# The mixer's output projection as seven products of block sums instead of eight block products

## The chip, the cores and the metric

One core of a Trainium2 chip runs the whole program. The metric is device time in microseconds (us) of that core. The kernel before was run three times: 1793.5, 1794.19 and 1794.78 us, median 1794.19 us. Each number of the trace comes from one profiled execution of its own.

## The reference, cut to what matters

Two layers of an encoder over 512 tokens with 1024 features, in f32. The change touches the one line marked in this cut; the lines around it say what is made before it and used after it.

```python
def reference(x, p, w_in, ...):
    h = x
    for i in range(DEPTH):
        u = rms_norm(h, norm_mix_pre[i])
        ...
        merged = (jax.nn.sigmoid(gate_a) * (att @ w_att_out[i])
                  + jax.nn.sigmoid(gate_b) * (ret @ w_ret_out[i]))
        h = h + rms_norm(merged @ w_out[i], norm_mix_post[i])      # the projection of the change
        u = rms_norm(h, norm_mlp_pre[i])
        ff = jnp.square(jax.nn.relu(u @ w_mlp_up[i])) @ w_mlp_down[i]
        h = h + rms_norm(ff, norm_mlp_post[i])
        gate = jax.nn.sigmoid(rms_norm(h) @ w_ple_gate[i])
        h = h + gate * rms_norm(p[i] @ w_ple_proj[i], norm_ple[i])
    return h
```

`merged` is 512 tokens x 1024 features, `w_out[i]` is 1024 x 1024.

## The kernel before, in words

**Precision.** Every f32 operand of a matmul is kept as two parts, a high part (rounded to the type that TensorE multiplies, made by a copy on ScalarE) and a low part (the rest, made by a subtraction on VectorE or GpSimd). A product takes three matmuls (high by high, high by low, low by high: `HL`, line 295).

**Weights.** All weights lie in HBM as chunks of 128 x 1024 numbers (512 KB). `PLAN_LAYER` (line 69) writes out the order of the chunks of a layer; `_items` (line 93) turns it into the items that TensorE uses. `prefetch` (line 271) prepares up to three items ahead of the one in use: SyncE's queue loads the chunk (`raw`, line 254), ScalarE makes the high part (line 278), VectorE or, for some kinds, GpSimd in two halves, the low part (line 301). Five tiles `wt` hold prepared items, so a new one can be begun when the item five before it has been used. Where an item is a sum of two blocks (so far only in the MLP's down projection, which already is done as seven products), `total` (line 260) loads one block with SyncE's queue into a tile and adds the other with an accumulating DMA that GpSimd issues (line 268). Raw chunks sit in four tiles of the tag "R", sums in two tiles of the tag "X".

**Order.** TensorE's instructions run in the order in which the program gives them. Those of the other engines are put in order by the scheduler, by priority, which is the place in the program; what is wrapped in `soon` (line 375) gets a higher one. Each engine then works its list in that order. `step` (line 325) counts pieces of work of TensorE, six matmuls each in the stages of interest, and after a fixed count (`AGE` 7, `AGE_PP` 8) puts waiting transposes into TensorE's order.

**The stage of the change (lines 753 to 777).** The eight feature tiles of `merged`, transposed, lie in `fb`; each gets its last addend from GpSimd (line 752). They are split into `uT` (lines 753 to 755). Then `row_job` (line 332) makes the left 512 columns of the product for all four token tiles (`ALL`), and then the right 512 columns one token tile after another (`ONES`): 192 matmuls of 512 columns. `evac_wo` (line 761) takes each result out of PSUM: sum of squares on ScalarE, product with the gain on VectorE. When a token tile t is complete, `pre_norm` (line 393) makes the norm's factor (two small GpSimd operations, lines 359 and 361), the residual (two VectorE operations, line 773), two sums of squares on ScalarE, another factor on GpSimd and the normalized rows `un` (two VectorE operations, line 406). Its `rest` (line 408) transposes `un` on TensorE in two PSUM banks of the tag "tp", of which there are two in all, and splits them into `uT` again (ScalarE line 416, VectorE line 417).

**After it.** `pp` (lines 786 to 797): 48 matmuls of 512 columns in eight pieces that don't need the norm, evacuated in turn by VectorE and ScalarE (`pn`). Then the first three chunks of the MLP's up projection, first for tokens 0 to 255 and then for 256 to 511 (`early`, lines 862 to 875), which do need `uT` of those tokens.

```python
    def row_mm(ps, ch, j, lhs, k, t, first, last):
        for n, (a, b) in enumerate(HL):
            nc.tensor.matmul(ps, lhsT=lhs(a, k, t), rhs=ch[:, b, j * S:(j + 1) * S],
                             start=first and n == 0, stop=last and n == 2)

    def step(age=None):
        clock[0] += 1
        age = AGE if age is None else age
        if pending and clock[0] - pending[0][0] >= age:
            soon(pending.pop(0)[1])()
        tick()
```

## Time and profile before

| what | value |
|---|---|
| three runs, median | 1794.19 us |
| profiled execution: its time | 1794.64 us |
| profiled execution: span of the trace | 1792.9 us |
| TensorE (PE) busy, matmuls | 1772.4 us (99% of the span), 8209 |
| VectorE (DVE) busy | 1145.4 us (64%) |
| ScalarE (ACT) busy | 807.5 us (45%) |
| GpSimd (POOL) busy | 382.6 us (21%) |
| DMA | 274.58 MB, mean 153 GB/s |

The time of the execution is 1.7 us above the span, which runs from the first to the last instruction. PE's granted clock is at its full level in all slices of the span. The rows name tiles by the program's names: `wt` prepared weights, `raw` and `wsum` weights on their way, `acc`, `s` and `tp` PSUM banks (and `acc` also the stage's result in SBUF), `un` normalized rows, `uT` transposed operands, `fT` the tiles of `merged`. A row of the timeline gives the start, the duration, engine, line, operation, tiles, count, and in brackets how long the engine was idle before and what released it.

### The profile page before, as it was taken

How to read it: one execution, taken by the hardware profiler on the slowest of the kernel's cores; microseconds unless marked ns; L12 is line 12 of the kernel's file. 1: busy time of each engine (PE TensorE's matmuls, PEld its weight loads, DVE VectorE, ACT ScalarE, POOL GpSimd, SP SyncE). 2: the span in 40 equal slices, each digit the busy share in tenths (PEclk: the TensorE clock that was granted, in tenths of full speed). 3: DMA queues.
4: the chain of work that ended last, by engine and by line, in shares of the span. 5: the costliest groups of instructions: out<-in, count | busy, mean ns of one | idle time of the engine just before them, and what ended most of it. 6: DMA issues, size and time to landing. Idle time of an engine off the chain costs nothing.

```text
span 1792.9 us, 22127 instructions
## 1 busy us (share of the span) xinstructions
PE 1772.4 (99%) x8209; PEld 1466.2 (82%) x8209; DVE 1145.4 (64%) x1803; ACT 807.5 (45%) x1271; POOL 382.6 (21%) x354
## 2 busy tenths in 40 slices
PE   8999999999999999999999999999999999999998
PEld 6888788888898888888788887888888888888887
DVE  6676777743465677674656767677444657667754
ACT  4255444332466454433443555444333664444342
POOL 2312244311142001002123222442012410000030
PEclk9999999999999999999999999999999999999999
DMA  5555464552347655552346545555422566664421
GB/s 213 194 193 159 149 212 137 166 175 95 117 142 188 165 158 161 156 184 70 129 141 214 165 145 172 184 159 187 136 101 99 165 170 156 169 175 130 165 71 60
DMA packets 87807, 274.58 MB, mean 153 GB/s; under 512 B 11921, under 2 KB 20497, under 8 KB 87698
## 3 DMA queue, kind: packets, MB, share of 16 engines
q1 hardware_dynamic: 80786, 247.99, 40.7%
q0 software_dynamic: 6912, 25.17, 8.3%
q8 instruction: 65, 1.06, 0.2%
q14 instruction: 44, 0.36, 0.1%
HBM read 239.55 MB, written 33.55 MB: 152 GB/s over the span
## 4 chain that ended last, share of the span: by engine, by line
PE 89%; DVE 4%; POOL 2%; ACT 2%; issue 1%; DMA 1%; SPq 0%; POOLq 0%; ACTq 0%
PE acc L312 28%; PE acc L322 19%; PE s L312 18%; PE acc L849 8%; PE tp L849 4%; PE tp L612 2%; PE tp L544 2%; PE tp L507 2%; PE acc L871 1%; PE tp L413 1%; POOL wt L301 1%; PE s L525 1%; PE s L526 1%; PE s L590 1%; PE s L871 1%
## 5 line engine op out<-in xcount | busy, mean ns | idle before, releaser
L312 PE MATMUL acc<-uT,wt 128*128 128x512 f32 x1920 | 472.8, 392 | 0.0
L312 PEld LDWEIGHTS acc<-uT,wt 128*128 128x128 f32 x1920 | 356.2, 188 | 71.8
L301 DVE TENSOR_TENSOR wt<-raw,wt 128x1024 fp32r<-128x1024 f32 x217 | 279.4, 1292 | 187.6 <-ACT wt L278 187.1
L278 ACT ACTIVATE wt<-raw 128x1024 fp32r<-128x1024 f32 x280 | 293.9, 1055 | 223.0 <-PE acc L312 114.0
L322 PE MATMUL acc<-wt,uT 128*128 128x512 f32 x1320 | 320.8, 396 | 4.4 <-ACT uT L416 1.8
L312 PE MATMUL s<-uT,wt 128*128 128x512 f32 x1392 | 323.7, 389 | 0.0
L312 PEld LDWEIGHTS s<-uT,wt 128*128 128x128 f32 x1392 | 261.1, 188 | 54.1
L322 PEld LDWEIGHTS acc<-wt,uT 128*128 128x128 f32 x1320 | 245.6, 189 | 55.6 <-DVE uT L417 2.6
L301 POOL TENSOR_TENSOR wt<-raw,wt 128x512 fp32r<-128x512 f32 x126 | 173.2, 1395 | 408.1 <-ACT wt L278 339.1
L849 PE MATMUL acc<-wt,op 128*128 128x512 f32 x672 | 159.5, 389 | 0.0
L849 PEld LDWEIGHTS acc<-wt,op 128*128 128x128 f32 x672 | 126.1, 188 | 26.2
L268 POOL DMA_DIRECT2D wsum<-in_w_dram x48 | 42.8, 900 | 420.1 <-DVE wt L301 141.0
L892 ACT ACTIVATE relu<-s 128x512 f32<-128x512 f32 x60 | 35.7, 595 | 180.7 <-PE s L312 172.0
L860 DVE TENSOR_TENSOR sumP<-acc,sumP 128x512 f32<-128x512 f32 x92 | 61.8, 686 | 56.4 <-PE acc L849 56.1
L312 PE MATMUL acc<-retT,wt 128*128 128x512 f32 x384 | 89.3, 389 | 0.0
L322 PE MATMUL acc<-wt,ff 128*128 128x512 f32 x384 | 88.5, 390 | 0.0
L301 DVE TENSOR_TENSOR wt<-wsum,wt 128x1024 fp32r<-128x1024 f32 x48 | 60.6, 1263 | 41.7 <-ACT wt L278 41.7
L312 PEld LDWEIGHTS acc<-retT,wt 128*128 128x128 f32 x384 | 72.1, 188 | 15.0
L322 PEld LDWEIGHTS acc<-wt,ff 128*128 128x128 f32 x384 | 71.8, 188 | 14.8
L304 ACT ACTIVATE rt<-rz 128x512 fp32r<-128x512 f32 x64 | 40.3, 631 | 91.5 <-DVE rz L594 91.0
L849 PE MATMUL tp<-wt,op 128*128 128x512 f32 x336 | 80.7, 389 | 0.0
L849 PEld LDWEIGHTS tp<-wt,op 128*128 128x128 f32 x336 | 63.1, 188 | 13.1
(165 smaller groups left out, 2153.5 us busy)
## 6 DMA issues: line engine op xcount, KB each, us to landing
raw<-in_w_dram SPq DMA_DIRECT2D x280, 512.0 KB, 3.7
wsum<-in_w_dram POOLq DMA_DIRECT2D x48, 512.0 KB, 5.5
kk<-stk SPq DMA_DIRECT2D x128, 128.0 KB, 3.8
wsum<-in_w_dram SPq DMA_DIRECT2D x24, 512.0 KB, 3.3
stq<-rr SPq DMA_DIRECT2D x16, 512.0 KB, 3.4
qs<-stq SPq DMA_DIRECT2D x128, 64.0 KB, 2.9
stk<-rr SPq DMA_DIRECT2D x16, 512.0 KB, 3.0
stv<-vr SPq DMA_DIRECT2D x16, 512.0 KB, 4.4
```

The source lines that it names most:

```text
L268: nc.gpsimd.dma_start(r, rows(src[1]), accum_op=ALU.add)
L278: nc.scalar.activation(t[:, 0, :], r, AF.Copy)
L301: eng.tensor_tensor(dst, src, hi.bitcast(F32), op=ALU.subtract)
L304: nc.scalar.activation(dst[:, 0], src, AF.Copy, scale=scale)
L312: nc.tensor.matmul(ps, lhsT=t[:, a, (off + k) * P:(off + k + 1) * P], rhs=r, start=k == 0 and n == 0, stop=k == kts - 1 and n == 2)
L322: nc.tensor.matmul(ps, lhsT=lhs(a, k, t), rhs=ch[:, b, j * S:(j + 1) * S], start=first and n == 0, stop=last and n == 2)
L507: nc.tensor.matmul(o, lhsT=v, rhs=pt[k][:, hl, :], start=k == 0 and hl == 0, stop=k == 3 and hl == 1)
L544: nc.tensor.transpose(ps[:, t * P:(t + 1) * P], zs[t][:, k * P:(k + 1) * P], ident)
L612: nc.tensor.matmul(o, lhsT=v[:, k, a * P:(a + 1) * P], rhs=rt[k][:, b, :], start=n == 0, stop=n == 11)
L849: nc.tensor.matmul(ps, lhsT=op[:, a, k, j * P:(j + 1) * P], rhs=t[:, b, k * S:(k + 1) * S], start=k == 0 and n == 0, stop=k == 1 and n == 2)
L860: nc.vector.tensor_tensor(a, ps, a, op=ALU.add)
L871: nc.tensor.matmul(early[c][:, 256 * j:256 * j + 256], lhsT=t[:, a, k * P:(k + 1) * P], rhs=uT[:, b, k, 256 * j:256 * j + 256], start=k == ...
```

## The change

The 512 x 1024 operand and the 1024 x 1024 weight are cut into two by two blocks, and the product is made as seven products of sums of blocks where eight block products were summed. Per layer and product: two items of weights (q), each used by twelve matmuls of 512 columns for two token tiles (j): 168 matmuls. The sums of weight blocks are made by accumulating DMAs as in the down projection; the first sum (P5) is kept in "R" tiles and grows into P6 and P4. The sums of the operand's blocks are made by VectorE (x, y, z, v), each operand is split (`wo_operand`), four of them into `uT`. The results are combined by VectorE in `evac_wo`. Tokens 256 to 511 (t = 2, 3) are complete after the sixth product (P4), tokens 0 to 255 after the seventh (P2). The early part of the up projection takes the second token half first.

```diff
-    + [("wo", c) for c in range(8)]
+    + [("wo", c) for c in (0, 1, 4, 5, 6, 7, 2, 3)]
...
+            if kind == "wo":
+                if c == 0:
+                    b11, b21, b12, b22 = ([CHUNK[i, "wo", 2 * b + q] for q in range(2)] for b in range(4))
+                    out += [((i, "wo" + p, q), tuple(b if b == "chain" else b[q] for b in src)) for p, src in (
+                        ("P1", (b11,)), ("P5", (b11, b12)), ("P6", ("chain", b22)), ("P7", (b12, b22)),
+                        ("P3", (b22,)), ("P4", ("chain", b21)), ("P2", (b21,))) for q in range(2)]
+                continue
...
     def total(key, src):
+        at = key[2] if key[1][:2] == "wo" else "sum"
         if src[0] == "chain":
-            r = chain["sum"]
+            r = chain[at]
         else:
-            r = blk("X", [P, D], name="wsum")
+            held = key[1][-2:] == "P5"
+            r = blk("R" if held and at != "sum" else "X", [P, D], name="wsum")
             nc.sync.dma_start(r, rows(src[0]))
-            if key[1] == "P5":
-                chain["sum"] = r
+            if held:
+                chain[at] = r
         nc.gpsimd.dma_start(r, rows(src[1]), accum_op=ALU.add)
...
-        for c in range(8):
-            src = fb[c // 2][:, c % 2, :]
-            split(uT[:, :, c, :], src)
...
+        def wo_operand(x, q, src, at=None):
+            if at is None:
+                at = blk("P", [P, 2, 2, 256], F32R, name="wop")
+            nc.scalar.activation(at[:, 0], src, AF.Copy)
+            nc.vector.tensor_tensor(at[:, 1], src, at[:, 0].bitcast(F32), op=ALU.subtract)
+            wop[x, q] = at
+
+        f1, f2 = fb[:2], fb[2:]
+        lo_k, hi_k = ([uT[:, :, 4 * kh + 2 * q:4 * kh + 2 * q + 2, :] for q in range(2)] for kh in range(2))
...
+        def sum_x(q, o):
+            nc.vector.tensor_tensor(o, f2[q][:, :, 256:], f1[q][:, :, 256:], op=ALU.subtract)
...
+        def sum_z(q, o):
+            nc.vector.tensor_tensor(o, f1[q][:, :, :256], f1[q][:, :, 256:], op=ALU.subtract)
...
+        def sum_y(q, o):
+            nc.vector.scalar_tensor_tensor(o, wx[q], -1.0, f1[q][:, :, :256], op0=ALU.mult, op1=ALU.subtract)
...
+        def sum_v(q, o):
+            nc.vector.scalar_tensor_tensor(o, wy[q], -1.0, f2[q][:, :, :256], op0=ALU.mult, op1=ALU.subtract)
...
+        for q in range(2):
+            wo_operand("P1", q, f1[q][:, :, :256], lo_k[q][:, :, :, :256])
+        wx = sums(sum_x)
+        wy = sums(sum_y)
+        for q in range(2):
+            wo_operand("P5", q, wx[q], lo_k[q][:, :, :, 256:])
+            wo_operand("P6", q, wy[q])
+        wz = sums(sum_z)
+        for q in range(2):
+            wo_operand("P7", q, wz[q])
+        wv = sums(sum_v)
+        for q in range(2):
+            wo_operand("P3", q, wv[q])
+        for q in range(2):
+            wo_operand("P4", q, f2[q][:, :, 256:], hi_k[q][:, :, :, 256:])
+        for q in range(2):
+            wo_operand("P2", q, f2[q][:, :, :256], hi_k[q][:, :, :, :256])
...
-        row_job([(i, "wo", c) for c in range(4)], u_lhs, evac_wo(0))
-        row_job([(i, "wo", 4 + c) for c in range(4)], u_lhs, evac_wo(1), ONES)
+        def done_wo(t, hf, src, eng):
+            hs_ = HALVES[hf]
+            ssq[t][hf] = sumsq(src, t2("junk"), None if hf else 1e-6)
+            eng.tensor_tensor(acc[t][:, hs_], src, g_post[:, hs_], op=ALU.mult)
+            if not hf:
+                pre_norm(h[t], t, g_pre, residual(t, acc, rstd_of(*ssq[t])))
...
+        @soon
+        def evac_wo(x, j, ps):
+            (l1, r1), (l2, r2) = ([a[:, sl] for sl in HALVES] for a in (acc[j], acc[2 + j]))
+            if x == "P1":
+                nc.scalar.activation(l1, ps, AF.Copy)
+            elif x == "P5":
+                w5.append(ps)
+            elif x == "P6":
+                nc.vector.tensor_tensor(l2, ps, l1, op=add)
+                nc.vector.tensor_tensor(r1, w5[j], l2, op=add)
+            elif x == "P7":
+                nc.vector.scalar_tensor_tensor(r2, ps, -1.0, r1, op0=ALU.mult, op1=ALU.subtract)
+                nc.vector.tensor_tensor(l2, ps, l2, op=add)
+                done_wo(2 + j, 1, r2, nc.gpsimd)
+            elif x == "P3":
+                nc.vector.scalar_tensor_tensor(r1, ps, -1.0, r1, op0=ALU.mult, op1=ALU.subtract)
+                done_wo(j, 1, r1, nc.gpsimd)
+            elif x == "P4":
+                nc.vector.tensor_tensor(l2, ps, l2, op=add)
+                done_wo(2 + j, 0, l2, nc.vector)
+            else:
+                nc.vector.tensor_tensor(l1, ps, l1, op=add)
+                done_wo(j, 0, l1, nc.vector)
+
+        w5 = []
+        wo_banks = [bank(tag) for tag in ("acc", "acc", "s", "s", "acc", "acc")]
+        for m, pr in enumerate(("P1", "P5", "P6", "P7", "P3", "P4", "P2")):
+            pss = [wo_banks[(2 * m + j) % 6] for j in range(2)]
+            for q in range(2):
+                t = chunk(i, "wo" + pr, q)
+                for j in range(2):
+                    for k in range(2):
+                        for n, (a, b) in enumerate(HL):
+                            nc.tensor.matmul(pss[j], lhsT=wop[pr, q][:, a, k, j * P:(j + 1) * P], rhs=t[:, b, k * S:(k + 1) * S],
+                                             start=q == 0 and k == 0 and n == 0, stop=q == 1 and k == 1 and n == 2)
+                    if q:
+                        evac_wo(pr, j, pss[j])
+                    step()
...
-        for j in range(2):
+        for j in (1, 0):
             settle(PAIRS[j])
             for c in range(EARLY):
-                if not j:
+                if j:
                     early.append(bank(EARLY_BANKS[c]))
```

## Rows read from the trace of the kernel before

**Rows 1.** Page part 1: engine, busy us, share of the span, instructions.

```profile
PE 1772.4 (99%) x8209; PEld 1466.2 (82%) x8209; DVE 1145.4 (64%) x1803; ACT 807.5 (45%) x1271; POOL 382.6 (21%) x354
```

**Rows 2.** Chain that ended last: the projection in either layer (start, us, what).

```profile
460.62 35.36 PE acc L322 x156
...
1347.28 35.36 PE acc L322 x156
```

**Rows 3.** Busy us by stretch, layer 1: projection, pp, early; PEclk, DMA share, GB/s.

```profile
core 0: us, PE busy (x) PEld busy (x) DVE busy (x) ACT busy (x) POOL busy (x), PEclk, DMA share, GB/s
460.50:505.80 45.30, 45.30 (x210) 37.67 (x209) 20.48 (x34) 19.17 (x39) 12.14 (x17) 1.00 0.27 98
505.80:518.50 12.70, 12.70 (x66) 10.69 (x65) 12.18 (x18) 7.90 (x16) 1.78 (x5) 1.00 0.70 248
518.50:535.80 17.30, 17.30 (x146) 17.30 (x145) 6.99 (x11) 8.57 (x14) 10.23 (x8) 1.00 0.32 99
```

**Rows 4.** Timeline of PE, layer 1: last product before, projection, transposes.

```profile
455.02 5.60 PE L312 MATMUL acc<-retT,wt 128*128 128x512 f32 x24
460.46 35.52 PE L322 MATMUL acc<-wt,uT 128*128 128x512 f32 x156
495.82 1.03 PE L413 MATMUL tp<-ident,un 128*128 128x128 f32 x8
496.61 5.73 PE L322 MATMUL acc<-wt,uT 128*128 128x512 f32 x24
502.19 1.03 PE L413 MATMUL tp<-ident,un 128*128 128x128 f32 x8
...
509.88 1.03 PE L413 MATMUL tp<-ident,un 128*128 128x128 f32 x8
...
516.23 1.03 PE L413 MATMUL tp<-ident,un 128*128 128x128 f32 x8
```

**Rows 5.** Timeline of DVE, layer 1: norms of the last token tiles.

```profile
499.35 1.28 DVE L417 TENSOR_TENSOR uT<-tp,uT 128x512 fp32r<-128x512 f32 x2
...
505.92 1.42 DVE L406 SCALAR_TENSOR_TENSOR un<-h,rstd,gain 128x512 f32<-128x512 f32 x2 [2.94 <-POOL rstd L361]
507.25 1.28 DVE L417 TENSOR_TENSOR uT<-tp,uT 128x512 fp32r<-128x512 f32 x2
508.44 1.22 DVE L301 TENSOR_TENSOR wt<-raw,wt 128x1024 fp32r<-128x1024 f32 x1
509.58 0.68 DVE L766 TENSOR_TENSOR acc<-acc,gain 128x512 f32<-128x512 f32 x1
510.18 1.41 DVE L773 SCALAR_TENSOR_TENSOR h<-acc,rstd,h 128x512 f32<-128x512 f32 x2
511.50 1.22 DVE L301 TENSOR_TENSOR wt<-raw,wt 128x1024 fp32r<-128x1024 f32 x1
...
513.78 1.42 DVE L406 SCALAR_TENSOR_TENSOR un<-h,rstd,gain 128x512 f32<-128x512 f32 x2 [0.40 <-POOL rstd L361]
515.12 1.28 DVE L417 TENSOR_TENSOR uT<-tp,uT 128x512 fp32r<-128x512 f32 x2
...
520.38 1.28 DVE L417 TENSOR_TENSOR uT<-tp,uT 128x512 fp32r<-128x512 f32 x2
```

**Rows 6.** Timeline of ACT: sum of squares that opens the norm of t=1 and t=3.

```profile
493.30 0.60 ACT L351 ACTIVATE junk<-acc 128x512 f32<-128x512 f32 x1 [1.63 <-PE acc L322]
...
506.21 0.59 ACT L351 ACTIVATE junk<-acc 128x512 f32<-128x512 f32 x1
```

**Rows 7.** Timeline of POOL: last addend of the operand; low part of a weight.

```profile
461.83 2.29 POOL L752 TENSOR_TENSOR fT<-m,fT 128x512 f32<-128x512 f32 x1 [9.92 <-DVE m L751]
...
502.16 2.94 POOL L301 TENSOR_TENSOR wt<-raw,wt 128x512 fp32r<-128x512 f32 x2 [0.91 <-ACT wt L278]
```

**Rows 8.** Page parts 5 and 6: high parts, accumulating DMAs, their time to landing.

```profile
L278 ACT ACTIVATE wt<-raw 128x1024 fp32r<-128x1024 f32 x280 | 293.9, 1055 | 223.0 <-PE acc L312 114.0
...
L268 POOL DMA_DIRECT2D wsum<-in_w_dram x48 | 42.8, 900 | 420.1 <-DVE wt L301 141.0
...
wsum<-in_w_dram POOLq DMA_DIRECT2D x48, 512.0 KB, 5.5
```

More of the change, by code (lines that the diff above doesn't have):

```diff
@@ L752, in one_layer @@
             nc.gpsimd.tensor_tensor(fb[c // 2][:, c % 2, :], m, fb[c // 2][:, c % 2, :], op=ALU.add)
-        for c in range(8):
-            src = fb[c // 2][:, c % 2, :]
-            split(uT[:, :, c, :], src)
         g_post, g_pre = gain_row(5 * i + 1), gain_row(5 * i + 2)
+        wop = {}
+        def wo_operand(x, q, src, at=None):
[4 more added lines that the diff above has]
+            wop[x, q] = at
@@ new lines, in one_layer, with sums @@
+        f1, f2 = fb[:2], fb[2:]
+        lo_k, hi_k = ([uT[:, :, 4 * kh + 2 * q:4 * kh + 2 * q + 2, :] for q in range(2)] for kh in range(2))
+        def sums(f):
+            return [f(q, t2("ws").rearrange("p (s n) -> p s n", s=2)) for q in range(2)]
+        def sum_x(q, o):
+            nc.vector.tensor_tensor(o, f2[q][:, :, 256:], f1[q][:, :, 256:], op=ALU.subtract)
+            return o
+        def sum_z(q, o):
+            nc.vector.tensor_tensor(o, f1[q][:, :, :256], f1[q][:, :, 256:], op=ALU.subtract)
+            return o
@@ new lines, in sum_y @@
+        def sum_y(q, o):
+            nc.vector.scalar_tensor_tensor(o, wx[q], -1.0, f1[q][:, :, :256], op0=ALU.mult, op1=ALU.subtract)
+            return o
+        def sum_v(q, o):
+            nc.vector.scalar_tensor_tensor(o, wy[q], -1.0, f2[q][:, :, :256], op0=ALU.mult, op1=ALU.subtract)
+            return o
+        for q in range(2):
[5 more added lines that the diff above has]
+            wo_operand("P6", q, wy[q])
@@ L758, in one_layer @@
+        wz = sums(sum_z)
[8 more added lines that the diff above has]
+            wo_operand("P2", q, f2[q][:, :, :256], hi_k[q][:, :, :, :256])
         acc = [blk("V", [P, D], name="acc") for _ in range(NT)]
         ssq = [[None, None] for _ in range(NT)]
-        def evac_wo(hf):
-            @soon
-            def f(t, ps):
-                hs_ = HALVES[hf]
-                ssq[t][hf] = sumsq(ps, t2("junk"), None if hf else 1e-6)
-                nc.vector.tensor_tensor(acc[t][:, hs_], ps, g_post[:, hs_], op=ALU.mult)
-                if hf:
-                    pre_norm(h[t], t, g_pre, residual(t, acc, rstd_of(*ssq[t])))
-            return f
+        LH, RH = HALVES
@@ L774, in residual @@
             return upd
-        row_job([(i, "wo", c) for c in range(4)], u_lhs, evac_wo(0))
-        row_job([(i, "wo", 4 + c) for c in range(4)], u_lhs, evac_wo(1), ONES)
+        def done_wo(t, hf, src, eng):
[4 more added lines that the diff above has]
+                pre_norm(h[t], t, g_pre, residual(t, acc, rstd_of(*ssq[t])))
+        add = ALU.add
```

## The prediction, made before the changed kernel ran

> **What bounds the kernel now.** I read the busy table of the page first: TensorE (PE) is busy for 99% of the span with 8209 matmuls [rows 1], so fewer matmuls are worth their full price only where nothing else makes PE wait. The chain that ended last says the same of this stage: in both layers it runs through the projection's matmuls without a break, 156 of them in 35.36 us [rows 2], or 0.2267 us each; a piece of six is 1.36 us. The windows by stretch show what lies beside them: in the projection VectorE (DVE) works 20.5 of 45.3 us, in the early up projection 7.0 of 17.3, but in the pp stretch between them 12.18 of 12.7 [rows 3]. There DVE is full already, with the norms of the last token tiles, and PE doesn't wait only because pp needs no norm. PE's timeline shows the transposes of the four tiles 6.4, 7.7 and 6.4 us apart [rows 4], each group costing PE 0.79 us (495.82 to 496.61). Layer 2 has the same pattern, so everything below counts twice.
>
> **The gain.** 192 matmuls become 168 per layer: 24 x 0.2267 = 5.44 us, 10.88 us in all. If nothing waits, the profiled execution's 1794.64 us becomes 1783.8.
>
> **What DVE gets per layer.** In DVE's timeline one 512-column operation follows another after 0.60 us (509.58 to 510.18), a weight's low part takes 1.14 (508.44 to 509.58), two residuals 1.32 (510.18 to 511.50), two `un` 1.34 (513.78 to 515.12) [rows 5]. Added: 8 block sums (4.8 us), 14 low parts of operands in place of 8 (3.6), 6 more weight items (6.8), 14 additions of products (8.4); four gain products go to GpSimd (-2.4). That is 21.2 us more. The three stretches together hold 39.65 us of DVE work in 75.3 us [rows 3]; they would hold 61 in 70. It fits on average; the question is when.
>
> **The head: nothing.** P1 and the first half of P5 need only tiles that are finished before the last product of `ro` ends (460.46) [rows 4]. P5's second item needs the last addend, which GpSimd finishes at 461.83 + 2.29 = 464.1 [rows 7]; a sum, a high part and a low part are about 1.9 us, so 466.0. It is due after 36 matmuls, 468.6. Cover 2.6 us; without it each us late is one lost.
>
> **The middle: nothing, with a risk.** From about 469 to 491.7 a weight item falls due every 2.72 us, 42% of DVE, and ten additions take 6.0 of 22.7 us, another 26%. PSUM banks are reused three products later, against additions of 1.2 us per tile. ScalarE gets 6 high parts of weights at 1.055 us [rows 8], 6 of operands and 2 copies, about 11 us more beside 19.2 of 45.3 [rows 3]. GpSimd gets 8 accumulating DMAs at 0.9 us [rows 8] and 4 gain products, between 1.3 and 2.3 us each (two such pieces in 2.94, one addend in 2.29) [rows 7]: 12 to 16 us beside 12.1. Ten more transfers of 512 KB on the DMA side (SyncE's queue 10 loads for 8) bring the projection from 98 to about 243 GB/s; the pp stretch moves 248 without a wait of PE [rows 3]. The risk is P6's second item: its sum is added onto P5's, so P5's second item must be split first. Its slot opens at 455.0 [rows 4]. If its split runs in a gap by 463, accumulating (0.9 + 5.5 to landing) [rows 8] and splitting (1.06 + 1.14) give 471.6, and it is due at 474.1 after 60 matmuls. If DVE does all 22 operations on operands first (13.2 us), it is 476.8: 2.7 us lost. I take nothing, since at least five of the 22 must wait for the last addend and leave a gap.
>
> **The tail: where the gain goes.** Before, token tiles became complete 5.44 us apart. Now t = 2 and 3 come after 138 and 144 matmuls (491.7, 493.1) and t = 0 and 1 after 162 and 168 (497.2, 498.5). The step counter puts the transposes of t = 2 seven pieces after its end (501.3), of t = 3 one piece and one group later (503.4), t = 0 at 508.3, t = 1 at 510.4. So they are asked for 2.15, 4.87 and 2.15 us apart. Four waits follow.
>
> T2. Before, from the sum of squares of t = 1 to its `un` it took 6.05 us (493.30 to 499.35), for t = 3 on the full DVE 8.9 (506.21 to 515.12) [rows 5, 6]. Now an addition comes first (0.8 with the handover), and t = 3's operations push in between (up to 2.5). That is 6.9 to 12.2 against 9.5 us: lost 0 to 2.7. I take 0.9, nearer the low end, since GpSimd's work on the pp weights, which held t = 2 up by 2.94 us before [rows 5, 7], should now be over by about 494.
>
> T3. Each group fills both "tp" banks, and the next may begin only when DVE has made the low parts out of them. From transposes to the end of the low parts it took 4.8, 6.3, 6.5 and 5.4 us before (the L413 rows against the L417 rows, each with its 1.28) [rows 4, 5], 5.75 on average, hidden by the wide spacing. Undisturbed it would be about 1.9 us (half a group, one high part, one low part, handovers). Against 2.15 us: lost 0 to 4.4. DVE is in the midst of the chains of t = 0 and 1, as in the rows, so I take 5.75 - 2.15 = 3.6.
>
> T0. Same bank wait against 4.87 us: 0 to 1.6 lost; I take 0.9.
>
> T1. Same against 2.15 us: 0 to 4.4 lost. By now DVE has only one chain left besides copies and weights that come behind in priority; I take 0.8.
>
> Sum 6.2 us per layer; bounds 0 and 13.1. A ledger of DVE checks the low side: from 491.9 to 510.4 are 18.5 us, and it must by then have done four chains (two additions or products, two residuals, two `un`, small ones: 3.98 each, 15.9), six low parts out of "tp" (3.6) and one `pn` copy (0.6): 20.1 us. Even a DVE that never idled would make PE wait 1.6 us. Early needs the second half's `uT` and then the first's 8.6 us later, so the new order there costs nothing; its first weight's low part has to fit in as well, another 1.1 us.
>
> [...]
>
> **Net.** 6.2 - 5.44 = +0.76 us per layer, +1.5 in all: 1796.1 for the profiled execution. That execution was 0.45 us above the median of the three runs, so against the median 1794.19 + 1.5 = 1795.7. A measurement of this kernel can tell about 0.2%, 3.6 us, from no change.
>
> **The rivals.**
> A, the forecast: the tail costs 3.6 to 7.2 us per layer, so 1790.6 to 1797.8, no change that can be told. For it: the measured bank times against the new spacing. Chance 0.40.
> B, faster: DVE is fed almost without gaps and T3 is served early, with a wait of 2.5 us per layer (the ledger's 1.6 and 0.9 of idle time): 1794.19 - 5.9 = 1788.3. For it: chains of four tiles in flight give DVE something to do at any time, and low parts from "tp" could be put ahead of t = 0 and 1. Against: DVE's order is fixed beforehand, and it was idle for 2.94 us amid such work [rows 5]. Chance 0.25.
> C, slower: the two "tp" banks decide at both close pairs. T2 waits 2.7, T3 3.6, T0 0.9, T1 3.6: 10.8 per layer, 1794.19 + 10.7 = 1804.9. It decides from a tail wait of 7.2 us per layer. For it: before, no group's low parts were done in under 4.8 us. Against: behind T0 the chains run out. Chance 0.25.
> D, slower: A, and P6's second weight late by 2.7 us per layer: 1795.7 + 5.4 = 1801.1. Against: the gap before the last addend. Chance 0.10.
> That it doesn't do what it says can be left out: 48 matmuls go whatever the engines do.
>
> **The numbers.** Likeliest is A, 1795.7. Faster 0.25 (B), same 0.40 (A), slower 0.35 (C and D). The range takes in A, D, a little over half of B and of C: 1788.0 to 1805.0; below lies the tail wait near the ledger's floor, above that all groups wait as long as the longest before. A's own range is 1790.6 to 1797.8.
>
> **What the profile after would show.** 8161 matmuls. Right: PE unbroken from P1 to P2's end, 38.1 us, then gaps at the transposes (L413 now) released by DVE's or ScalarE's `uT` operations or by `un`, of 6 us per layer, the longest at the second group; DVE over 95% busy from P4's end to the start of early; no PE gap in early. Wrong: no gap at the second group (B), gaps over 3 us at the fourth (C), or a gap inside the products, at P6's second item above all, released by a weight's low part (D). A wait of the norm's factors behind an accumulating DMA on GpSimd would be a cause that I have priced nowhere.

## The result and the profile after

The changed kernel takes **1825.34 us** (median of 4 runs, 1824.06 to 1826.67) against 1794.18 us for the kernel before beside it: ratio 1.0175, 95% interval 1.0162 to 1.0188. It is slower by 31 us, above the whole range. The profiled execution took 1826.67 us, its span is 1824.9 us.

Part 1 of the page of the changed kernel, as [rows 1]:

```profile
PE 1773.1 (97%) x8161; PEld 1460.2 (80%) x8161; DVE 1193.1 (65%) x1863; ACT 827.6 (45%) x1299; POOL 409.4 (22%) x378
```

The 48 matmuls are gone, but PE is busy as long as before: some of the remaining ones ran at a lower granted clock (0.50 in the last row below). VectorE has 47.7 us more, 23.9 per layer. Busy times by stretch, layer 1, as [rows 3]: P1 to P2's end, from there to early, and one pp piece of the second:

```profile
core 0: us, PE busy (x) PEld busy (x) DVE busy (x) ACT busy (x) POOL busy (x), PEclk, DMA share, GB/s
461.30:502.20 40.90, 38.74 (x169) 31.20 (x167) 35.90 (x45) 23.61 (x38) 14.63 (x11) 1.00 0.65 168
502.20:534.70 32.50, 19.50 (x82) 14.23 (x82) 24.30 (x42) 15.90 (x36) 11.15 (x19) 0.79 0.48 175
510.40:513.30 2.90, 2.88 (x6) 1.81 (x6) 2.17 (x5) 0.00 (x0) 1.76 (x3) 0.50 0.84 278
```

Before, P1's place to early took 58.0 us in either layer; now 73.3 (461.32 to 534.66) and in layer 2 74.1 (1363.34 to 1437.42). That is 15.3 + 16.1 = 31.4 us, the whole difference. No engine is full: VectorE works 24.3 of the last 32.5 us. The timeline of PE, as [rows 4], says where it stood:

```profile
461.32 5.60 PE L865 MATMUL acc<-wt,uT 128*128 128x512 f32 x24
...
468.82 5.30 PE L865 MATMUL s<-wt,uT 128*128 128x512 f32 x22 [1.44 <-DVE uT L771]
...
477.78 8.27 PE L865 MATMUL acc<-wt,wop 128*128 128x512 f32 x35 [0.72 <-DVE wt L310]
...
491.33 11.04 PE L865 MATMUL acc<-wt,uT 128*128 128x512 f32 x48
510.42 2.90 PE L331 MATMUL acc<-wt,phl 128*128 128x512 f32 x6 [8.05 <-DVE acc L853]
515.27 2.93 PE L331 MATMUL acc<-wt,phl 128*128 128x512 f32 x6 [1.95 <-DVE ss L362]
...
521.98 1.26 PE L422 MATMUL tp<-ident,un 128*128 128x128 f32 x8 [1.08 <-DVE uT L426]
...
528.48 1.26 PE L422 MATMUL tp<-ident,un 128*128 128x128 f32 x8 [1.12 <-DVE uT L426]
...
532.19 1.25 PE L422 MATMUL tp<-ident,un 128*128 128x128 f32 x8 [0.80 <-DVE uT L426]
...
534.66 3.03 PE L963 MATMUL s<-uT,wt 128*128 128x256 f32 x24
```

2.2 us are lost in the head (P5, P6), 8.05 and 1.95 ahead of the first two pieces of pp, which need no norm, and only 3.0 at the transposes. Behind the long gap a piece of six matmuls takes 2.90 us, at a granted clock of 0.50 (1.63 us at 1.00, from 519.26).

Why pp waited: its first two pieces take the PSUM banks of P2, and those come free with P2's additions (L853). VectorE's timeline, as [rows 5]:

```profile
500.55 0.15 DVE L362 TENSOR_SCALAR ss<-ss 128x1 f32<-128x1 f32 x1 [2.88 <-ACT junk L360]
...
505.93 1.41 DVE L820 SCALAR_TENSOR_TENSOR h<-acc,rstd,h 128x512 f32<-128x512 f32 x2 [4.42 <-POOL rstd L370]
507.26 2.35 DVE L310 TENSOR_TENSOR wt<-raw,wt 128x1024 fp32r<-128x1024 f32 x2
...
509.60 0.68 DVE L853 TENSOR_TENSOR acc<-acc,acc 128x512 f32<-128x512 f32 x1
510.68 0.75 DVE L415 SCALAR_TENSOR_TENSOR un<-h,rstd,gain 128x512 f32<-128x512 f32 x1 [0.41 <-POOL rstd L370]
```

The addition's data were there by 502.4, when P2's last matmul ended, but in VectorE's order it stands behind the residual of t = 2, and that waited 4.42 us for the norm's factor. The chain of work that ended last shows what the factor stood behind, GpSimd's pp weights and a gain product, and behind those a late chunk:

```profile
488.54 8.64 DMA raw<-in_w_dram
497.28 1.07 ACT wt L287
...
500.96 1.69 POOL acc L826
502.65 2.44 POOL wt L310 x2
505.10 0.16 POOL rstd L368
```

**The stage in three parts.** The summary of the eight `un` operations of layer 1 (two per token tile; first and last start), before and after:

```profile
L406 DVE SCALAR_TENSOR_TENSOR un<-h,rstd,gain x8: 745/749/752, 492.6 to 514.5; 128x512 f32<-128x512 f32 x8
```

```profile
L415 DVE SCALAR_TENSOR_TENSOR un<-h,rstd,gain x8: 745/749/754, 510.7 to 530.8; 128x512 f32<-128x512 f32 x8
```

The stretch from P1 to early is the time to the first `un`, from there to the last, and the rest to early. With the values of the runs below, and with the time that VectorE is busy from the first `un` to early:

| kernel, layer 1 | to first un | first to last | rest | sum | VectorE, first un to early |
|---|---|---|---|---|---|
| before | 32.1 | 21.9 | 4.0 | 58.0 | 20.6 |
| after | 49.4 | 20.1 | 3.9 | 73.3 | 19.9 |
| e4, operands early | 45.1 | 20.1 | 3.9 | 69.1 | 19.9 |
| d1, no low parts of weights | 41.2 | 20.1 | 3.9 | 65.2 | 19.9 |
| e6, paired chains | 51.5 | 12.5 | 11.9 | 75.8 | 21.0 |
| n1, no waits for factors | 47.8 | 17.0 | 8.0 | 72.8 | 21.8 |
| h1, factors on ScalarE and VectorE | 49.2 | 20.6 | 3.9 | 73.7 | 20.3 |
| v10, four edits and a new order | 45.4 | 16.4 | -3.6 | 58.2 | 11.8 |

The rows behind the last column for before, after and n1 (columns as in the windows above):

```profile
492.60:518.47 25.87, 25.87 (x131) 21.73 (x131) 20.60 (x32) 16.42 (x34) 7.57 (x14) 1.00 0.46 169
```

```profile
510.70:534.66 23.96, 19.02 (x80) 13.89 (x80) 19.90 (x36) 12.11 (x28) 6.78 (x12) 0.83 0.44 162
```

```profile
514.80:539.78 24.98, 18.74 (x80) 15.28 (x81) 21.82 (x40) 15.68 (x36) 0.00 (x0) 0.80 0.61 203
```

Before, the 25.9 us from the first `un` to early cost nothing, because they were full of TensorE's work. Now this part is about as long (24.0 us, VectorE busy 19.9), but TensorE has only 14.0 us of work left for it (eight pieces of pp and four groups of transposes), and it starts 17.3 us later: 4.1 us since the first tile is complete after 138 matmuls and not 120 (18 x 0.2267), 2.8 in the products ahead (2.2 of them as waits of PE), and 10.4 because the way from the last matmul of P4's first tile (495.4) to its `un` takes 15.3 us where it took 4.9 (487.7 to 492.6).

### The profile page after: what moved, and what is told of

The parts are those of the page before. It is cut to its first block, busy times and chain, and to the rows that moved or that the text cites. A ratio compares the mean times of both kernels' runs of the same rounds, so it can differ in the third digit from the quotient of the medians.

```text
span 1824.9 us, 22243 instructions
## 1 busy us (share of the span) xinstructions
PE 1773.1 (97%) x8161; PEld 1460.2 (80%) x8161; DVE 1193.1 (65%) x1863; ACT 827.6 (45%) x1299; POOL 409.4 (22%) x378
## 4 chain that ended last, share of the span: by engine, by line
PE 81%; DVE 7%; POOL 4%; ACT 3%; issue 2%; DMA 2%; SPq 0%; POOLq 0%; ACTq 0%; DVEq 0%
PE acc L321 26%; PE s L321 17%; PE acc L331 14%; PE acc L941 8%; PE tp L941 4%; PE tp L621 2%; PE tp L553 2%; PE tp L516 1%; POOL wt L310 1%; PE acc L963 1%; DVE wt L310 1%; POOL rstd L370 1%; DMA raw<-in_w_dram 1%; PE acc L865 1%; ACT un L360 1%
## 5 line engine op out<-in xcount | busy, mean ns | idle before, releaser
L310 DVE TENSOR_TENSOR wt<-raw,wt 128x1024 fp32r<-128x1024 f32 x213 | 271.5, 1282 | 171.6 <-ACT wt L287 171.1
L287 ACT ACTIVATE wt<-raw 128x1024 fp32r<-128x1024 f32 x276 | 289.8, 1055 | 205.9 <-PE acc L321 105.9
L331 PE MATMUL acc<-wt,uT 128*128 128x512 f32 x936 | 232.5, 398 | 5.1 <-ACT uT L425 2.2
L331 PEld LDWEIGHTS acc<-wt,uT 128*128 128x128 f32 x936 | 173.8, 190 | 41.6 <-DVE uT L426 2.9
L277 POOL DMA_DIRECT2D wsum<-in_w_dram x64 | 56.6, 892 | 490.5 <-DVE wt L310 163.3
L310 DVE TENSOR_TENSOR wt<-wsum,wt 128x1024 fp32r<-128x1024 f32 x64 | 87.8, 1379 | 43.4 <-ACT wt L287 43.3
L287 ACT ACTIVATE wt<-wsum 128x1024 fp32r<-128x1024 f32 x64 | 67.6, 1056 | 64.0 <-DMA wsum<-in_w_dram 28.7
```

Source lines behind the costliest of these rows:

```text
L277: nc.gpsimd.dma_start(r, rows(src[1]), accum_op=ALU.add)
L287: nc.scalar.activation(t[:, 0, :], r, AF.Copy)
L310: eng.tensor_tensor(dst, src, hi.bitcast(F32), op=ALU.subtract)
```

## Experiments

Each is an edit of the changed kernel. The kernel before, on the same chip, took 1794.1 to 1794.6 us beside them, and 1796.63 us beside d1, v9, v9g and v9g_4. Each edit but v10 was run once; v10's eleven runs spread over 5.4 us, so a difference of a few us between single runs decides nothing.

### Single places: e1 to e4

```diff
e1 -POOL_MORE = [("pp",0),("pp",1)]
   +POOL_MORE = []
e2 +        bank("acc"), bank("acc")
            praw = blk("A", [P, 2, S], name="praw")
e3 -            r = blk("R" if held and at != "sum" else "X", [P, D], name="wsum")
   +            r = blk("X" if held or at == "sum" else "R", [P, D], name="wsum")
e4 +            if c == 7:
   +                operands_wo((0,))
                ps = bank("acc")
                t_job((i, "ro", c), ps, rhs=retT)
```

In e4 the operands that need no tile finished by `ro`'s last product are issued ahead of it.

> The changed kernel with the low parts of the two pp weights on VectorE instead of GpSimd. Theory Q (GpSimd's queue): after the products PE waits 8 us because GpSimd works on the late pp weights (498.4 to 505.1) in front of the norm's factors of t = 2; without them the factor comes about 4 us earlier, so 3 to 5 us less per layer, 1815 to 1819 in all. Theory B (banks): PE waits since pp begins on the two PSUM banks of P2, whose additions stand late in VectorE's order; nothing changes by more than 2 us. Theory T (the prediction's: four norm chains and two transposing banks): no change, or 1 to 2 us per layer more, as VectorE gets 2.3 us more work.

> The changed kernel with the rotation of PSUM banks moved on by two before pp, so that its first two pieces write the banks of P4, which are free early. Theory B: the waits of 8.05 and 1.95 us at these pieces go, PE keeps its clock, and the transposes of t = 2 then wait for the rows to be normalized: about 5 us less per layer, 1815. Theory Q: the same factor on GpSimd is waited for one place later; the two pieces (2.7 us) slip ahead of it, 2 to 3 us less per layer, 1819 to 1821. Theory T: the same as Q.

> The changed kernel with the sums that are kept from P5 to P4 in the two tiles of the tag X, and P7's sums, which live shortly, in the tiles R of the raw chunks. Theory Q, with late raw chunks as the cause of GpSimd's late work: raw chunks of P2 and pp load from about 470 instead of 484 to 497, the pp weights' low parts are done before the first norm, 4 to 6 us less per layer, 1813 to 1817. Theories B and T: no change beyond 2 us.

> The changed kernel with the operands that don't need the last feature tile (P1, P7, and the first item of the other five) emitted before the last product of ro instead of after it. All theories: the two gaps at P5 and P6 (1.44 and 0.72 us) go, 2 us less per layer. If the burst of operand work on VectorE (463 to 476) is what makes the weights, and with them the raw tiles and GpSimd's work, late, another 3 to 6 us per layer go: 1809 to 1815. If not (B and T): 1820 to 1822.

Measured: e1 1831.01, e2 1826.11, e3 1824.08, e4 **1816.97** us. e1 and e2 lie outside every expectation, e3 is what theories B and T said, e4 falls between its two. In e2 pp did begin at once (500.99), and the same time was then lost at the transposes, the first of them 6.65 us: pp's wait was only where PE met the late norms first. In e1 VectorE and ScalarE stood still for the late chunks in GpSimd's place: ScalarE 2.97 us for a load (up to 497.33), VectorE 3.10 us for ScalarE's high part of it (up to 498.43). Only e4 gained, 4.3 us in the stretch, all of it in the time to the first `un`: the head's waits (2.2) go, and the way from P4 to that `un` is 2.1 us shorter.

### Pairs, and everything off GpSimd: e6, c1345, c13456

```diff
e6 -                pre_norm(h[t], t, g_pre, residual(t, acc, rstd_of(*ssq[t])))
   +            if not hf and t % 2:
   +                norm_pair((t - 1, t))
c1345 (e1, e3, e4 and)
   -                done_wo(2 + j, 1, r2, nc.gpsimd)
   +                done_wo(2 + j, 1, r2, nc.vector)
   -                done_wo(j, 1, r1, nc.gpsimd)
   +                done_wo(j, 1, r1, nc.vector)
c13456 (c1345 and e6)
```

> The changed kernel with one edit: the norm chains of the two tiles of a pair are emitted stage by stage side by side (residual of both, sums of both, factors of both, un of both) and not one whole chain after the other. Theory (the four chains run one after another because each engine's order is fixed and every stage of the later tile stands behind the round trip of the earlier one; un came 6.5 us apart): within a pair un should come about 1.3 us apart, the stretch from the last product's end to early shrinks by 4 to 8 us per layer, 1810 to 1817 us; the 8 us gap ahead of pp stays, since the first factor is as late as before. Rival (VectorE simply has too much work in that stretch, 24.3 us of it): the chains only change places, 1822 to 1828 us.

> Four edits together: the pp weights' low parts on VectorE instead of GpSimd, the gain products on VectorE instead of GpSimd, the sums for P5 in the tiles of X and those for P7 in the tiles of R, and the operands that need no last tile emitted before ro's last product. The last alone gave 1817. Theory (the gap ahead of pp is the late first norm factor, queued on GpSimd behind 6.7 us of pp weights and gain products): with GpSimd free the factor comes at about 497 instead of 501 to 505, the gap of 5.9 us falls to 1 to 3, 1805 to 1811 us. Rival (the raw chunks of pp's weights are late, and whichever engine splits them stands still in its fixed order): no better than the early operands alone, 1815 to 1825 us.

> The four edits of the run before it and the paired norm chains. Theory (late factor and serial chains are two separate causes and add up): both savings, 1795 to 1804 us. Rival (VectorE's work is the floor of this stretch, and each edit puts more on it): no better than the better of the two single ones, 1808 us or more.

Measured: 1830.67, 1817.5, 1816.11 us, against 1816.97 with e4 alone: e6 is slower than either side expected, the other two are the rivals' numbers. Pairing did bring `un` closer (12.5 us from first to last), but the first came later and early began 11.9 us after the last: 24.4 us from the first `un` to early, about as in the changed kernel. In c1345 the gap ahead of pp fell, as expected, and returned at the transposes. PE's timeline of c1345:

```profile
501.73 1.61 PE L331 MATMUL acc<-wt,phl 128*128 128x512 f32 x6 [1.18 <-DVE acc L858]
...
510.53 1.32 PE L422 MATMUL tp<-ident,un 128*128 128x128 f32 x8 [2.25 <-DVE un L415]
...
519.37 0.66 PE L422 MATMUL tp<-ident,un 128*128 128x128 f32 x4 [1.81 <-DVE un L415]
...
523.89 2.93 PE L331 MATMUL acc<-wt,phl 128*128 128x512 f32 x6 [2.01 <-DVE pn L893]
```

So GpSimd's queue held up most of the gap ahead of pp (8.05 us in the changed kernel, 5.89 in e4, 1.18 here), but taking its work away paid nothing, since it went to VectorE: the first `un` came 2.1 us sooner than in e4, and from it to early it took 25.9 us (VectorE busy 21.3) and no longer 24.0 (19.9).

### Is it the waiting, or VectorE's amount of work? n1 and d1

```diff
n1 -        r = rstd_of(*sq)
   +        r = fixed if upd and gain is not None else rstd_of(*sq)
   -                pre_norm(h[t], t, g_pre, residual(t, acc, rstd_of(*ssq[t])))
   +                pre_norm(h[t], t, g_pre, residual(t, acc, fixed))
d1 -            for sl in HALVES if pool else (slice(0, D),):
   +            for sl in () if key[1][:2] == "wo" else HALVES if pool else (slice(0, D),):
   -   rhs=t[:, b, k * S:(k + 1) * S],
   +   rhs=t[:, 0, k * S:(k + 1) * S],
```

> The changed kernel with one part of the computation replaced: the eight norm factors of this stage (two for each token tile, in both layers) are a constant tile and are not computed, so that no residual and no un waits for GpSimd. Sums of squares, products, additions, residuals and un stay, so VectorE's large operations are the same. Theory (the loss is waiting: each tile needs two round trips VectorE, ScalarE, GpSimd, VectorE, and what stands behind them in each engine's fixed order waits along): the 8 us gap ahead of pp and most of the gaps at the transposes go, 10 to 15 us less per layer, 1796 to 1806 us. Rival (VectorE has too much work between P2's end and early, 24.3 us of it): PE still waits for it, 1815 us or more.

> The changed kernel with one part of the computation left out: the low parts of the projection's fourteen weight items are not computed, and the third matmul of each triple takes the high part in their place (168 matmuls as before). VectorE has 14 operations of 1.14 us less per layer, 16 us; the waits for factors, the sums of products, the transfers and the transposes stay. Theory (VectorE has more work in this stretch than TensorE, 60 against 52 us, and every order only moves the wait): the stretch from P1 to early falls from 73 to 58 to 62 us, 1796 to 1803 us. Rival (the round trips of the four chains set the length, 6.5 us from one un to the next): the head's two waits go and little else, 1817 to 1823 us.

n1: **1845.94 us**, slower than the changed kernel by 21 us with no factor to wait for, where the theory said faster by 20 to 30; the rival's "1815 us or more" holds. Its VectorE timeline:

```profile
496.55 1.77 DVE L823 SCALAR_TENSOR_TENSOR h<-acc,fixed,h 128x512 f32<-128x512 f32 x1 [2.72 <-POOL acc L829]
498.24 1.21 DVE L310 TENSOR_TENSOR wt<-wsum,wt 128x1024 fp32r<-128x1024 f32 x1
```

Without the factors, residuals were put ahead of weights that the products still needed; here P4's weight stands behind a residual that waits 2.72 us for GpSimd's gain product, and PE now waits for weights inside the products (1.33, 0.71 and 0.87 us from 498 to 510). P1 too began later than in the changed kernel (466.95 against 461.32). The edit changed the order of VectorE's whole list, so its time doesn't decide between waiting and work. Its last part says more: with no factor to wait for, the four tiles' `un` still take 17.0 us from first to last, and it is 25.0 us from the first to early, with VectorE busy for 21.8 of them.

d1: **1811.19 us**, 14.6 above the kernel before beside it, where the changed kernel is 31 above: 20.7 us of VectorE's busy time less per layer (1151.7 us in all, against 1193.1) gave back 8.2 us per layer. Between the two expectations. Its `un` operations, and busy times from P1 to P2's end and from there to early:

```profile
L415 DVE SCALAR_TENSOR_TENSOR un<-h,rstd,gain x8: 744/749/754, 503.4 to 523.5; 128x512 f32<-128x512 f32 x8
```

```profile
462.20:500.40 38.20, 38.20 (x169) 31.34 (x167) 24.03 (x38) 24.80 (x37) 16.20 (x15) 1.00 0.73 200
500.40:527.40 27.00, 18.18 (x82) 13.21 (x81) 22.52 (x40) 14.70 (x35) 7.55 (x14) 0.87 0.48 177
```

The products now run unbroken in 38.2 us, and the first `un` comes 8.2 us sooner. But from the first to the last it is 20.1 us again, to the tenth the same as after and in e4. This doesn't clear VectorE's amount of work of that interval: the fourteen low parts that d1 leaves out all lie ahead of the first `un`, and behind it VectorE has the same 19.9 us of work to early in all three kernels. What the missing work moved is the time to the first `un`: SyncE's loads of raw chunks resume at 476.0 and not at 483.7, GpSimd has the pp weights and the gain product between them from 491.0 to 497.8 and not from 498.4 to 505.1, and the factor that the first residual needs is begun 35.6 us after P1's start and not 43.7. VectorE's and ScalarE's timelines of d1 show what the interval is made of, here for the second tile of the four (t = 3) and the third (t = 0):

```profile
505.90 1.41 DVE L820 SCALAR_TENSOR_TENSOR h<-acc,rstd,h 128x512 f32<-128x512 f32 x2 [0.44 <-POOL rstd L370]
...
509.83 1.42 DVE L415 SCALAR_TENSOR_TENSOR un<-h,rstd,gain 128x512 f32<-128x512 f32 x2 [0.72 <-POOL rstd L370]
511.16 0.15 DVE L362 TENSOR_SCALAR ss<-ss 128x1 f32<-128x1 f32 x1
...
512.62 1.42 DVE L820 SCALAR_TENSOR_TENSOR h<-acc,rstd,h 128x512 f32<-128x512 f32 x2 [0.71 <-POOL rstd L370]
...
516.34 1.42 DVE L415 SCALAR_TENSOR_TENSOR un<-h,rstd,gain 128x512 f32<-128x512 f32 x2 [1.04 <-POOL rstd L370]
```

```profile
506.69 0.63 ACT L360 ACTIVATE un<-h 128x512 f32<-128x512 f32 x1 [3.72 <-DVE h L820]
...
507.98 0.61 ACT L360 ACTIVATE junk<-acc 128x512 f32<-128x512 f32 x1
```

Residual, `un`, the next tile's residual, its `un`: 6.5 to 6.7 us per tile, each step released by a factor. P2's addition for t = 0 was done at 503.0, but ScalarE's sum of squares of it (507.98) stands in its list behind the two sums over the residual of t = 3, which waited 3.72 us, and the small addition to it on VectorE (511.16) behind the `un` of t = 3. A tile's first step thus waits, in two lists, for the last steps of the tile before, and the chains run one behind the other. But of the 20.1 us VectorE works 16.0 and waits only 4.1 for factors; the work in the list is the larger part.

### A different order: v7_46 and its variants

```diff
v7 -    + [("wo", c) for c in (0, 1, 4, 5, 6, 7, 2, 3)]
   -    + [("pp", c) for c in range(2)]
   +    + [("wo", c) for c in (0, 1, 4, 5, 6, 7)] + [("pp", 0)] + [("wo", c) for c in (2, 3)] + [("pp", 1)]
   ...
   +            if pr == "P2":
   +                pp_half(0)
   +            pss = [wo_banks[(2 * m + j) % 6 if pr != "P2" else 2 + j] for j in range(2)]
   ...
   +        pp_half(1)
   -AGE_PP = 8
   +AGE_PP = 10
a12 AGE_PP = 12; "4", "5", "6" are the edits of e4, of c1345's gain products, of e6; "3" that of e3
v9  v7_46 and POOL_MORE = [("pp",0)]
v9g v9 and all pn copies by nc.scalar.activation; v9g_4 without e6
```

> Early operands, paired chains, and the pp products moved: pp's first half between P4 and P2, its second half after P2, P2 on the two banks that scores use, so that no pp piece waits for a bank whose addition stands behind a norm. Theory (PE waits because all four norm chains come after the last work that needs no norm): with 5.4 us of pp work behind t = 2 and 3's last sum and 5.4 behind that of t = 0 and 1, the stretch loses 3 to 6 us per layer against a PE without waits, so 1789 to 1796 us, the seven products' 10.9 us just about kept or lost. Rival (VectorE's work is the floor): the waits only move to the transposes, 1805 us or more.

> Early operands, gain products on VectorE, pp's first half between P4 and P2 and its second half after P2, as in the run that gave 1805.7, but chains not paired, and the transposes of t = 2 and 3 two pieces of six matmuls later (2.7 us). Theory (there the transposes were asked for 1.9 us before un was there, and the factor stood 3 us behind pp's second weight and 7 us of gain products on GpSimd): 1795 to 1801 us. Rival (un comes later by as much, since VectorE's order moves along): 1804 us or more.

> The run before it with the chains of a pair emitted side by side. Theory (in a pair the second tile's work fills the first one's round trips): both un come before the transposes are asked for, 1792 to 1798 us. Rival (the pair makes the first tile wait for the second): up to 5 us more than unpaired.

> As the unpaired one, with the sums for P5 in the tiles of X and those for P7 in the tiles of R, so that the R tiles are free for the raw chunks of pp sooner. Theory (pp's weights are late because the R tiles are held): 1 to 3 us less than unpaired without it. Rival (the swap only moves the wait to P7's sums): the same or up to 3 us more.

> The kernel that gave 1805.7 (early operands, paired chains, pp's halves behind P4 and behind P2) with one edit: the low part of pp's second weight on VectorE instead of GpSimd, where the first norm factor stood 3 us behind it while VectorE was idle for 3.2 us. Theory (that factor is on the path there): 2 to 3 us less per layer, 1799 to 1802 us. Rival (the next wait, for the low parts out of the tp banks, is set by VectorE's work and stays): 1804 to 1808 us.

> The run before it with all eight pn copies per layer on ScalarE instead of half of them on VectorE: 2.4 us of VectorE's work less per layer. Theory (VectorE's work): 2 to 5 us less than the run before it in all. Rival (the copies lie in VectorE's idle time, or ScalarE's own sums of squares come later by them): the same or up to 3 us more.

> The run before it with the chains one after the other and not paired. Theory (in a pair the second tile's operations fill the first one's round trips): 3 to 10 us more than paired. Rival (pairing only delays the first tile): 2 to 5 us less.

Measured: v7_46 **1805.7** (11.2 above the kernel before), the three with later transposes 1816.4, 1815.64 and 1815.43, v9 1808.9 (12.3 above), v9g 1806.13 (9.5 above), v9g_4 1814.45 us. The first four are the rivals' numbers or, in v7_456_a12 and v7_345_a12, within 1 us of v7_45_a12; v9g and v9g_4 came out as their theories said. With later transposes, and the gain products on VectorE, it is 10 us worse: the two tp banks are then filled close together, and PE waits for their low parts (4.31 us in v7_45_a12). The swap of tiles is again worth no more than 1 us. In this order pairing is worth 8 us (v9g against v9g_4), where alone it lost 5. v9 missed: with the weight's low part off GpSimd, VectorE stood idle 2.48 us for ScalarE's high part of it.

### The round trips: h1 and v10

```diff
   +        if eng is nc.vector:
   +            nc.scalar.activation(r, a, AF.Sqrt, bias=b)
   +            nc.vector.reciprocal(r, r)
   +            return r
h1  the factors of this stage with eng=nc.vector
v10 v7_46, all pn copies on ScalarE, the factors of this stage with eng=nc.vector
```

> The changed kernel with one edit: the norm factors of this stage are made by a square root on ScalarE (with the other half's sum as bias) and a reciprocal on VectorE, in place of an addition and a power on GpSimd. Each round trip loses GpSimd's 1.1 to 1.5 us and one hand-over. Theory (the four chains run one behind the other, so un comes one chain's length apart): the distance from un to un falls from 6.5 to 4 to 5 us, 4 to 8 us per layer less, 1809 to 1817 us. Rival (places in VectorE's fixed order set the distance): 6 to 6.5 us as before, 1820 us or more.

> Early operands, paired chains, pp's halves behind P4 and behind P2, all pn copies on ScalarE, pp's weights on GpSimd as in the changed kernel, and the factors on ScalarE and VectorE. Theory (round trips): 2 to 4 us per layer less than the run with paired chains and copies on ScalarE (9.5 us above the kernel before on its chip), so 2 to 6 us above the kernel before. Rival (VectorE's work): 8 to 10 us above it. Under the kernel before it comes only if both round trips of a pair were on the path.

h1: 1826.7 us, nothing gained; the rival's number. From the first `un` to the last it was still 20.6 us (510.2 to 530.8): VectorE, which now makes the reciprocals, works 18.0 of them. v10: **1795.23 us** (median of 11 runs), the kernel before beside it 1794.08 (15 runs), ratio 1.0006 (0.9997 to 1.0015): no difference that can be measured, and a little better than the 2 to 6 us above it that were expected. PE's timeline of v10 (an execution of 1799.19 us):

```profile
509.42 1.38 PE L431 MATMUL tp<-ident,un 128*128 128x128 f32 x8 [0.91 <-DVE un L852]
...
513.27 0.66 PE L431 MATMUL tp<-ident,un 128*128 128x128 f32 x4 [1.07 <-DVE ss L363]
515.32 1.12 PE L431 MATMUL tp<-ident,un 128*128 128x128 f32 x4 [1.40 <-DVE uT L435]
...
521.40 3.04 PE L993 MATMUL s<-uT,wt 128*128 128x256 f32 x24
```

Of the 15.1 us by which its stretch is shorter than after's, 3.9 lie ahead of the first `un`, 3.7 between first and last, and 7.5 in the rest: early begins 3.6 us before the last `un`, because the second token half, which early takes first, is transposed by then, and the transposes of t = 0 and 1 lie inside early. The new order thus takes work out of the way of early: from the first `un` to early VectorE has 11.8 us to do and not 19.9.

## Why the prediction was wrong

**The gain** was right: 168 matmuls, and where nothing interrupts them 38.2 us (d1) against the 38.1 predicted.

**DVE +21.2 us per layer** measured 23.9. In layer 1 alone three weights took 1.1 us more each beside GpSimd's operations (2.31 us at 464.05 and 490.67, last section, and 3.45 for two at 487.30 where two took 2.35), two of them beside the gain products, whose move there I had booked as relief for VectorE.

**Head: nothing** was wrong by 1.44 us, but not at P5's second item: PE stood after two matmuls of its first item, for the low part of that item's operand. **The middle's risk** at P6's second item came true with 0.72 in layer 1 and not at all in layer 2. I had put the operands' work from 455 on; VectorE began P5's block sums at 463.4, behind pp's split, for whose load ScalarE had waited 3.34 us. Early operands alone (e4) removed both waits: PE ran from 461.48 to 500.40 without one.

**The tail** is the step that failed, and in it first of all T2. From P2's end at 502.3 to early PE lost 18.4 us in layer 1 (32.4 less 8 pieces of 1.36 and four groups of 0.79), where the forecast was 6.2 and the upper bound 13.1. T2 allowed 6.9 to 12.2 us from the end of t = 2's product to its `un`, "lost 0 to 2.7", because GpSimd's work on the pp weights "should now be over by about 494". Measured: that work, with a gain product in its midst, lay between 498.4 and 505.1, the norm's factor stood behind it, and `un` was done 17.3 us after the product (495.4 to 512.8). VectorE, which the ledger kept busy from 491.9 on, worked 6.7 of the 15.3 us to the first `un`. So the first group of transposes began 15.7 us after P2's end (13.6 in layer 2) and not 3.6 (two pieces of pp and the 0.9 of T2): 12.1 of the 12.2 us by which the tail was off in layer 1.

From the first group to early it took 16.7 us in layer 1, and the prediction's terms give 16.6. That is luck. T3, T0 and T1 priced the waits of groups that come soon after P2; where the first group did come sooner (e2, c1345), 23.8 and 24.8 us passed from it to early. What no term held is that about 20 us of VectorE's work and 4 us of waits for factors lie between the first `un` and early, in a fixed order, against 14.0 us of TensorE's. Before, this part was as long (25.9 us, VectorE 20.6) and covered. The ledger had work of that size (20.1 us), but let it begin at P4's end and run without gaps.

**Two reuses** that the prediction left out belong to it: pp's first two pieces take P2's banks, and P2's additions stand in VectorE's list behind the first residual. With banks of their own (e2) the time moved to the transposes, so this placed the loss and didn't cause it.

**The last sentence** feared a factor behind an accumulating DMA on GpSimd; it was behind pp's weights and a gain product (505.1). Taking these away was worth nothing where the work went to VectorE (c1345: 1817.5 us, e4 without it 1816.97).

**The rivals.** C came nearest in sign, by another size and place: it gave the waits at the transposes 10.8 us per layer, and these waits, released by `uT` as forecast, were 3.0 us in layer 1 and 4.7 in layer 2. In v7_45_a12, with its late transposes, one of them is 4.31 us. "DVE over 95% busy from P4's end" was wrong: 25.9 of 37.9 us. No PE gap in early: right.

Settled are the place of the loss; that the late work on GpSimd, which moves with VectorE's load ahead of it (d1), makes the first `un` late; and that 23 to 28 us pass from the first `un` to early in every kernel with the old order, with paired chains (e6), factors without GpSimd (h1) or no factors to wait for (n1). That VectorE's amount of work sets this last part is the likeliest reading and not shown: the one run that takes work off VectorE there and leaves the order alone, v9g, gained 2.8 us against v9, which single runs can't tell from nothing. Open is also how v10's last 8 us against v9g divide between its two edits, and whether an order exists that keeps any of the 10.9 us; none of these did.

## What to carry to other kernels

Here 24 fewer matmuls per layer made the kernel 31 us slower, because the dependent work behind them was no longer covered. Before moving completions to the end of a stage, read in the profile of before what lies between the first result that is ready and the first consumer (here 20 us of VectorE's work in 26 us), and compare it with the matmuls that will be left to cover it (here 14 us). A wait removed alone came back at a later place in the engines' fixed lists (in e2 8.05 us ahead of pp, then 6.65 at the transposes; the like in e1, e6, c1345 and h1). Early operands alone gave back 8 us; the time of the kernel before was reached only when start and order were changed together. Work that needs no norm belongs between the completions, and the consumer should begin with the tiles that are complete first.

## What the runs showed of the hardware

**VectorE beside GpSimd.** In the changed kernel two low parts of weights on VectorE took 2.31 us each beside an operation of GpSimd, where one took 1.23 with GpSimd idle (457.66). VectorE's and GpSimd's timeline:

```profile
464.05 2.31 DVE L310 TENSOR_TENSOR wt<-wsum,wt 128x1024 fp32r<-128x1024 f32 x1
...
490.67 2.31 DVE L310 TENSOR_TENSOR wt<-raw,wt 128x1024 fp32r<-128x1024 f32 x1
```

```profile
463.61 1.66 POOL L761 TENSOR_TENSOR fT<-m,fT 128x512 f32<-128x512 f32 x1 [3.49 <-DVE m L760]
...
487.99 3.91 POOL L826 TENSOR_TENSOR acc<-acc,gain 128x512 f32<-128x512 f32 x2
```

Both end 1.08 to 1.09 us after GpSimd's operation does (466.36 after 465.27, 492.98 after 491.90), the time of about one such low part, as if they had begun only then. In h1 two residuals took 3.23 us beside GpSimd's weight work (503.80), and 1.41 with GpSimd idle (518.44).

**The clock.** In layer 1, behind 8.05 us without a matmul, the granted clock was 0.50 from 510.4 to 518.0, and two pp pieces took 2.90 and 2.93 us where one took 1.63 at 1.00 (519.26); behind 1.08 us without a matmul, ahead of the second group of transposes, it was 1.00 (521.98 to 523.24). The two pieces so took about 2.6 us more than at 1.63 each. In layer 2, behind 7.23 us, the first piece took 2.90 us at 0.50, the second 1.65.

**A table load on ScalarE.** The first square root of the stage in h1 was preceded by a table load of 1.28 us, the seven others of layer 1 by none:

```profile
501.43 1.28 ACT L368 ACT_TABLE_LOAD   x1
```
